# A depthwise convolution shared by two engines: one-tap adds on GpSimd against adds four taps wide

## The chip, the cores and the metric

The kernel runs on one NeuronCore of one Trainium2 chip. The metric is the device time of one execution in microseconds. Three runs of the kernel before took 962.43, 964.1 and 961.76 us; their median is 962.43.

## The reference

A decoder trunk of two layers on 256 positions with 1024 channels, all in float32. Each layer adds half a gated feed-forward network (FFN), a token mixer, and half a second FFN to the residual x; the mixer of the first layer is a pair of convolutions, that of the second is attention. The change lies in the first layer's mixer:

```
def conv_mixers(h, w_in, a_kernel, b_kernel, b_bias, b_ln_g, b_ln_b, w_out):
    z = h @ w_in                                # 1024 -> 2560 channels
    a_b, a_c, a_x, b_val, b_gate = split(z)     # 512 channels each
    y_a = a_b * causal_depthwise_conv(a_c * a_x, a_kernel)          # 3 taps
    u = b_val * sigmoid(b_gate)
    u = causal_depthwise_conv(u, b_kernel) + b_bias                 # 31 taps
    y_b = silu(layer_norm(u, b_ln_g, b_ln_b))
    return concatenate([y_a, y_b]) @ w_out
```

The 31-tap convolution works on each of 512 channels by itself: for every position it is a sum of 31 products, one of each of the last 31 values of u with the channel's weight for that distance.

## The kernel before

Activations lie transposed: 128 channels on the partitions, 256 positions in the free dimension, so a set of 512 channels is four groups of 128x256. Weights come from memory in units of 16 tiles of 128x128 (1 MB, line 116, issued by SyncE), into four buffers. To multiply in float32 accuracy at the faster rate, each unit is split into a rounded part (ScalarE, line 127) and a remainder (VectorE, line 128), and each product is made of three matmuls (lines 163 to 165). A few units, named in WHOLE and the two units for ya, are not split and are used as they are, in a slower matmul (line 161). Such a unit keeps its buffer until TensorE has read it.

The convolution stage (function conv) runs over ten steps p. Each projects a pair of 128-channel groups into a PSUM bank. Steps 0 to 3 give value and gate of the 31-tap convolution, one group c each; VectorE and ScalarE make u[c] from them (lines 499 to 502). Steps 4 to 7 give the two factors of the 3-tap convolution (lines 515 to 529, result ya), steps 8 and 9 its outer gate (lines 538 and 539). Then the first half of the output projection multiplies ya (line 161, 64 matmuls), while the layer norm of the other half runs: sums of y over the channels (GpSimd and VectorE, line 561), a matmul with ones for the mean (line 563), subtraction (line 566), squares, a second matmul (line 201), the reciprocal root, its spreading (line 241), gain and SiLU (lines 576 and 578), and a split into two parts ob[0] and ob[1] (lines 187 and 188). The second half of the output projection multiplies ob.

The 31 taps of a group are shared out. VectorE takes the first 31 - POOL_TAPS[c]: the first as one multiply with the bias added (line 453), each further one as one multiply-and-add into a PSUM accumulator (line 464; the last group has a second accumulator, yl, line 460). For the other taps ScalarE makes the product of one tap (line 486, 128x256) in one of PBUFS = 18 buffers and GpSimd adds it to yp (line 487, 128x256); the first is written into yp by ScalarE itself (line 481). Line 473 adds the two parts into y[c], line 470 adds yl into yp.

The order of the work is written out by hand. Two lists, queue_v for VectorE's taps and queue_p for the products with their adds, get a group's entries when its u is there. At the end of step p, PER_POOL[p] entries of queue_p and then PER_STEP[p] of queue_v are put into the program; the closing addition of a group is placed LATE entries into the next group's taps. AHEAD says how far ahead of the projections units are split. A planner then orders each engine's instructions by this program order, in which a part of the layer norm is moved forward by PRIO_LN; after that each engine runs its queue strictly in order.

All tiles of the stage lie in a pool that is open for the stage alone; xg is a copy of the scaled input, read by the unsplit projections, and ob is a pair of tiles of its own.

Of the kernel before, what the change touches and what calls it, by code (L numbers as in the profile page):

```python
# [10 lines left out]
F32 = mybir.dt.float32  # L11
F32R = mybir.dt.float32r
I32 = mybir.dt.int32
AF = mybir.ActivationFunctionType
# [3 lines left out]
P = 128  # L18
D = 1024
S = 256  # L20
DEPTH = 2
FF = 2816
ND = D // P
# [6 lines left out]
KB = 31  # L30
# [3 lines left out]
UT = 16  # L34
NEG = -1e30

POOL_TAPS = [13, 17, 13, 16]
PER_STEP = [9, 8, 7, 8, 8, 8, 9, 8, 9, 10]
PRIO = 0
WHOLE = {9, 2}  # L40
PBUFS = 18
PER_POOL = [6, 8, 2, 6, 6, 9, 6, 4, 8, 9]
XPRIO = 0
AHEAD = [2, 4, 1, 1, 4, 4, 3, 4, 3, 3]
LATE = 15
OUT_AHEAD = [2, 3]
PRIO_LN = 800
WARM = 7
FINE = {13: 4, 14: 4, 6: 4}
PRIO_C = 500  # L50
PRIO_R = 500
# [9 lines left out]
LINE = 1024  # L61
# [33 lines left out]
def trunk(ctx: ExitStack, tc: tile.TileContext, xin, wst, cst, bia, idn, out):  # L95
    nc = tc.nc
# [21 lines left out]
    def split(u):  # L118
# [3 lines left out]
        w2[u] = w2s.tile([P, UT * P], F32R, name="w2")  # L122
        n = max(2, PIECES.get(u, 1), FINE.get(u - first_conv, 1))
        h = UT * P // n
# [29 lines left out]
    def take(n):  # L154
        st = Stream(used[0])
        used[0] += n
        return st
# [251 lines left out]
    def out_half(st, accs, half, o, ds, ahead=(ahead_split,) * 2):  # L409

        for d in ds:
            for k in range(4):
                t = half * 32 + d * 4 + k
                if t % UT == 0:
                    advance(st.u + t // UT, ahead[t // UT % 2])
                mm3(accs[d // 2][:, d % 2], st.tile(t), [a[:, k] for a in o],
                    half == 0 and k == 0 and d % 2 == 0, half == 1 and k == 3, True)
# [4 lines left out]

    def conv(norm, after):
        with tc.tile_pool(name="cp", bufs=1, reuse_waits="tile") as cp, \
                tc.tile_pool(name="cp2", bufs=PBUFS, reuse_waits="tile") as cp2:
            xg = cp.tile([P, ND, S], F32, name="xg")
            with tc.high_priority(offset=XPRIO):
                for k in range(ND):
                    nc.scalar.activation(xg[:, k], x[:, k], AF.Copy,
                                         scale=const[:, norm.col + k:norm.col + k + 1])  # L430
            _, r = norm.end(WIDEC)
            ob = [cp.tile([P, 4, S], F32R, name=f"ob{i}") for i in range(2)]
            u = cp.tile([P, 4, KB - 1 + S], F32, name="u")
            m = cp.tile([P, 4, KA - 1 + S], F32, name="m")
            y = cp.tile([P, 4, S], F32, name="y")
            yp = cp.tile([P, 4, S], F32, name="yp")
# [8 lines left out]
            def tap(c, j):  # L445
                return const[:, C_BK + c * KB + j:C_BK + c * KB + j + 1]

            def taps_v(c):

                acc = ys[c // 2][:, c % 2]  # L450

                def first():
                    nc.vector.tensor_scalar(acc, u[:, c, :S], tap(c, 0),
                                            const[:, C_BB + c:C_BB + c + 1],
                                            op0=ALU.mult, op1=ALU.add)
                yield first
                for j in range(1, KB - POOL_TAPS[c]):
                    def one(j=j):
                        if c in TWO and j == 1:
                            nc.vector.tensor_scalar_mul(yl[:, TWO.index(c)], u[:, c, j:j + S],  # L460
                                                        tap(c, j))
                            return
                        o = yl[:, TWO.index(c)] if c in TWO and j % 2 else acc
                        nc.vector.scalar_tensor_tensor(o, u[:, c, j:j + S], tap(c, j), o,  # L464
                                                       op0=ALU.mult, op1=ALU.add)
                    yield one

                def last():
                    if c in TWO:
                        nc.vector.tensor_add(yp[:, c], yp[:, c], yl[:, TWO.index(c)])  # L470
                    while any(a <= c for a, _ in queue_p):
                        queue_p.pop(0)[1]()
                    nc.vector.tensor_add(y[:, c], yp[:, c], acc)
                yield last

            def taps_p(c):

                j0 = KB - POOL_TAPS[c]

                def first():  # L480
                    nc.scalar.activation(yp[:, c], u[:, c, j0:j0 + S], AF.Copy, scale=tap(c, j0))
                yield first
                for j in range(j0 + 1, KB):
                    def one(j=j):
                        t = cp2.tile([P, S], F32, name="prod")
                        nc.scalar.activation(t, u[:, c, j:j + S], AF.Copy, scale=tap(c, j))  # L486
                        nc.gpsimd.tensor_add(yp[:, c], yp[:, c], t)  # L487
                    yield one

            queue_v, queue_p, late = [], [], None  # L490
            st = take(10)
            for p in range(10):
                advance(st.u + p, AHEAD[p])
                bank = project(st, p * UT, norm.xs, xg)
                c = p % 4
                with tc.high_priority(offset=PRIO):
                    if p < 4:
# [3 lines left out]
                        nc.scalar.activation(sg, v[:, 1], AF.Sigmoid)  # L501
                        nc.vector.tensor_mul(u[:, c, KB - 1:], v[:, 0], sg)
                        new = list(taps_v(c))
                        held_last, late = late, new.pop()
                        queue_v += new[:LATE] + [f for f in [held_last] if f] + new[LATE:]
                        queue_p += [(c, f) for f in taps_p(c)]
                    elif p < 8:
                        t = tmp.tile([P, S], F32, name="g")
# [5 lines left out]
                        else:  # L514
# [4 lines left out]
                                             scale=const[:, ka:ka + 1])  # L519
                        for j in range(1, KA):  # L520
                            w = const[:, ka + j:ka + j + 1]
                            if T_POOL[c]:
                                t = tmp.tile([P, S], F32, name="sl")
# [6 lines left out]
                    else:  # L530
                        c = 2 * (p - 8)
# [8 lines left out]
                if p == TABLE:  # L540
                    nc.scalar.activation(rsq[:, :1], m[:, 3, KA - 1:KA], AF.Silu)
                for _ in range(min(len(queue_p), PER_POOL[p])):
                    queue_p.pop(0)[1]()
                    if ROBIN and queue_p:
                        a = queue_p[0][0]
                        i = next((i for i, f in enumerate(queue_p) if f[0] != a), None)
                        if i is not None:
                            queue_p.insert(0, queue_p.pop(i))
                for _ in range(min(len(queue_v), PER_STEP[p])):
                    queue_v.pop(0)()  # L550
            for f in queue_v + [late]:
                f()

            st = take(4)
            accs = [psa.tile([P, 2, S], F32, name="pa") for _ in range(4)]
            out_half(st, accs, 0, [ya], range(8), OUT_AHEAD)
            with tc.high_priority(offset=PRIO_LN):
# [16 lines left out]
                _, rs = rsqrt_of([sq2], CM, LN_EPS)  # L574
                for c in range(4):
# [3 lines left out]
                                         scale=const[:, C_LG + c:C_LG + c + 1],  # L579
# [129 lines left out]
    for lo, hi in START:  # L709
        c = slice(2 * lo * P, 2 * hi * P)  # L710
# [4 lines left out]
    cold = psb.tile([P, P], F32, name="pb")  # L715
    for _ in range(WARM):
        nc.tensor.matmul(cold, ones, ones, start=True, stop=True)
# [13 lines left out]
    with tc.tile_pool(name="fp", bufs=1, reuse_waits="tile") as fp:  # L731
# [6 lines left out]
        _, r = rsqrt_of([last.sums, last.sq], D, RMS_EPS, eps)  # L738
        for i, (lo, hi) in enumerate(GROUPS):
            n = hi - lo  # L740
# [93 lines left out]
```

## Time and profile before

| | |
|---|---|
| median of three runs | 962.43 us (961.76 to 964.1) |
| the profiled execution | 960.91 us, of which the span of the trace is 958.8 |
| TensorE (PE) | busy 944.7 us, 99% |
| VectorE (DVE) | busy 731.8 us, 76% |
| ScalarE (ACT) | busy 548.9 us, 57% |
| GpSimd (POOL) | busy 47.9 us, 5%, 61 instructions |
| memory | 174.23 MB read, 183 GB/s over the span |

Engines run side by side, each through its own queue. A busy share is an average over stages with different limits: GpSimd's 5% lies almost wholly in one stretch of 50 us of the convolution stage, from about 204 to 258 us, where it is busy nine tenths of the time. A line of the timeline gives start, duration, engine, line, operation, what it writes and reads, how many instructions are merged, and in brackets how long the engine was idle before and who released it. Merged durations include what lies between the first start and the last end. A matmul's duration includes its way through the pipeline, so consecutive ones overlap.

### The profile page before, as it was taken

The numbers are of one execution on the slowest core, as the hardware profiler recorded it, in microseconds if no ns is written. First come the engines' busy times: TensorE is split into PE (matmuls) and PEld (weight loads), VectorE is DVE, ScalarE is ACT, GpSimd is POOL, SyncE is SP. The second block draws the span as 40 slices with busy tenths as digits, with TensorE's granted clock in tenths as the row PEclk, the third lists the DMA queues.
The fourth block names the chain that finished last, engine by engine and source line by source line (L and its number), as shares of the span: only waits on it lengthen the run. The fifth ranks groups of instructions, "written<-read, shape, count | busy, mean of one in ns | idle before, by whom it ended". The sixth has DMA issues, their size and how long they took to land.

```text
span 958.8 us, 15184 instructions
## 1 busy us (share of the span) xinstructions
PE 944.7 (99%) x5860; PEld 847.1 (88%) x5860; DVE 731.8 (76%) x1383; ACT 548.9 (57%) x985; POOL 47.9 (5%) x61
## 2 busy tenths in 40 slices
PE   9999999999899999999999999999999999999996
PEld 8988898999798888988988889898888998889886
DVE  8988776688999888766788877665698798787552
ACT  6665654497366665544466565444666565665540
POOL 0000000049600000000000000000000000000000
PEclk9999999999999999999999999999999999999998
DMA  9865565543175555555455555556553455555501
GB/s 337 290 213 177 184 212 176 191 161 133 45 284 186 203 204 176 187 209 176 176 201 195 178 197 197 179 201 212 187 198 123 157 184 189 200 194 179 200 17 44
DMA packets 27288, 176.26 MB, mean 184 GB/s; under 512 B 3024, under 2 KB 3792, under 8 KB 6864
## 3 DMA queue, kind: packets, MB, share of 16 engines
q1 hardware_dynamic: 26784, 174.67, 52.2%
q8 instruction: 46, 0.75, 0.3%
q10 hardware_dynamic: 432, 0.63, 0.2%
q14 instruction: 26, 0.21, 0.1%
HBM read 174.23 MB, written 1.05 MB: 183 GB/s over the span
## 4 chain that ended last, share of the span: by engine, by line
PE 91%; DVE 3%; ACT 2%; POOL 1%; issue 1%; DMA 0%; SPq 0%; DVEq 0%; POOLq 0%; ACTq 0%
PE pa L169 33%; PE pa L170 17%; PE pb L169 15%; PE pb L170 8%; PE pa L163 4%; PE pa L164 4%; PE pa L165 4%; PE pa L161 2%; ACT prod L486 1%; DVE pb L464 1%; PE pb L163 1%; PE pb L164 1%; PE pb L165 1%; POOL yp L487 1%; DVE w L128 1%
## 5 line engine op out<-in xcount | busy, mean ns | idle before, releaser
L128 DVE TENSOR_TENSOR w<-raw,w 128x1024 fp32r<-128x1024 f32 (+1 forms) x322 | 381.5, 1196 | 133.6 <-ACT w L127 133.0
L169 PE MATMUL pa<-xs,w 128*128 128x512 f32 x1376 | 479.1, 391 | 0.0
L127 ACT CAST w<-raw 128x1024 fp32r<-128x1024 f32 (+1 forms) x322 | 325.0, 1027 | 134.3 <-PE pa L169 50.0
L170 PE MATMUL pa<-xs,w 128*128 128x256 f32 x1376 | 387.6, 282 | 0.0
L169 PEld LDWEIGHTS pa<-xs,w 128*128 128x128 f32 x1376 | 258.3, 188 | 54.8 <-DVE xs L191 0.5
L170 PEld LDWEIGHTS pa<-xs,w 128*128 128x128 f32 x1376 | 260.0, 189 | 0.1
L169 PE MATMUL pb<-gs,w 128*128 128x512 f32 x616 | 213.7, 390 | 0.0
L170 PE MATMUL pb<-gs,w 128*128 128x256 f32 x616 | 173.7, 282 | 0.0
L169 PEld LDWEIGHTS pb<-gs,w 128*128 128x128 f32 x616 | 115.6, 188 | 24.1
L170 PEld LDWEIGHTS pb<-gs,w 128*128 128x128 f32 x616 | 116.4, 189 | 0.0
L386 ACT ACTIVATE sl<-v 128x256 f32<-128x256 f32 x88 | 36.8, 418 | 106.0 <-DVE v L341 102.0
L339 ACT COPY sq<-pa 128x256 f32<-128x256 f32 x172 | 63.3, 368 | 30.1 <-PE pa L170 24.9
L164 PE MATMUL pa<-xs,w 128*128 128x256 f32 x272 | 76.2, 281 | 0.1
L163 PE MATMUL pa<-xs,w 128*128 128x256 f32 x272 | 76.2, 282 | 0.0
L165 PE MATMUL pa<-xs,w 128*128 128x256 f32 x272 | 76.1, 280 | 0.0
L340 DVE TENSOR_TENSOR v<-pa,sq 128x256 f32<-128x256 f32 x156 | 65.1, 418 | 0.0
L405 DVE SCALAR_TENSOR_TENSOR x<-pb,x 128x256 f32<-128x256 f32 x60 | 25.4, 423 | 42.5 <-PE pb L170 28.5
L487 POOL TENSOR_TENSOR yp<-yp,prod 128x256 f32<-128x256 f32 x55 | 46.3, 845 | 207.8 <-ACT prod L486 203.8
L190 ACT ACTIVATE xs<-x,const 128x256 fp32r<-128x256 f32 x48 | 24.2, 506 | 54.8 <-DVE x L405 43.0
L341 DVE TENSOR_TENSOR v<-v,rr 128x512 f32<-128x512 f32 x78 | 53.4, 684 | 0.0
L164 PEld LDWEIGHTS pa<-xs,w 128*128 128x128 f32 x272 | 51.5, 189 | 0.5 <-DVE xs L191 0.3
L165 PEld LDWEIGHTS pa<-xs,w 128*128 128x128 f32 x272 | 51.1, 188 | 0.2 <-DVE w L128 0.2
(160 smaller groups left out, 926.5 us busy)
## 6 DMA issues: line engine op xcount, KB each, us to landing
raw<-wst SPq DMA_DIRECT2D x159, 1024.0 KB, 4.8
bt<-bia SPq DMA_DIRECT2D x8, 384.0 KB, 3.6
raw<-wst SPq DMA_DIRECT2D x7, 256.0 KB, 6.0
raw<-wst SPq DMA_DIRECT2D x2, 512.0 KB, 6.0
x<-xin SPq DMA_DIRECT2D x3, 256.0 KB, 4.9
out<-y SPq DMA_DIRECT2D x2, 256.0 KB, 2.5
out<-y ACTq DMA_DIRECT2D x2, 256.0 KB, 2.4
x<-xin SPq DMA_DIRECT2D x2, 128.0 KB, 3.1
```

Of the source, the lines that this page charges most:

```text
L127: nc.scalar.copy(w1[u][:, c], raw[u][:, c])
L128: nc.vector.tensor_sub(w2[u][:, c], raw[u][:, c], w1[u][:, c].bitcast(F32))
L163: nc.tensor.matmul(o, a[0], b[0], start=start, stop=False, skip_group_check=check)
L164: nc.tensor.matmul(o, a[0], b[1], start=False, stop=False, skip_group_check=check)
L165: nc.tensor.matmul(o, a[1], b[0], start=False, stop=stop, skip_group_check=check)
L169: nc.tensor.matmul(o, w[0], b, start=start, stop=False, skip_group_check=True)
L170: nc.tensor.matmul(o[:, 0], w[1], b[:, 0], start=False, stop=stop, skip_group_check=True)
L339: nc.scalar.copy(h, bank[:, 1])
L340: nc.vector.tensor_add(v[:, i], bank[:, 0], h)
L341: nc.vector.tensor_mul(v, v, twice(r))
L386: nc.scalar.activation(sl, v[:, 0], AF.Silu)
L487: nc.gpsimd.tensor_add(yp[:, c], yp[:, c], t)
```

## The change

- GpSimd's share is 18 of 31 taps in each group (before 13, 17, 13 and 16).
- ScalarE makes products four to a tile of 128x1024: the first four go straight into acc, four running sums; each further tile (three of four products, one of two) is added to acc by one GpSimd instruction, of 128x1024 or 128x512. A fold then adds the upper two sums to the lower two (128x512) and these to each other, into yp (128x256).
- There are 4 such product tiles (before 18 of one product each) and 2 of acc.
- queue_p has six entries a group; PER_POOL, PER_STEP and LATE have other values.
- In the closing step, the entries of queue_p are put into the program ahead of line 470's addition instead of behind it, since yp is now written by the fold.
- ob takes the buffer of xg, 960 bytes into it; xg's buffer is 1 KB a partition larger.

```
-POOL_TAPS = [13, 17, 13, 16]
-PER_STEP = [9, 8, 7, 8, 8, 8, 9, 8, 9, 10]
+POOL_TAPS = [18, 18, 18, 18]
+QUAD = 4
+PER_STEP = [6, 6, 5, 6, 6, 6, 6, 5, 5, 5]
-PBUFS = 18
-PER_POOL = [6, 8, 2, 6, 6, 9, 6, 4, 8, 9]
+PBUFS = 4
+PER_POOL = [3, 3, 2, 3, 3, 3, 3, 2, 2, 2]
-LATE = 15
+LATE = 10
+OB_START = 960
...
-            xg = cp.tile([P, ND, S], F32, name="xg")
+            xg = cp.tile([P, ND * S + LINE // 4], F32, name="xg")[:, :ND * S].rearrange(
+                "p (d s) -> p d s", d=ND)
...
-            ob = [cp.tile([P, 4, S], F32R, name=f"ob{i}") for i in range(2)]
...
                 def last():
+                    while any(a <= c for a, _ in queue_p):
+                        queue_p.pop(0)[1]()
                     if c in TWO:
                         nc.vector.tensor_add(yp[:, c], yp[:, c], yl[:, TWO.index(c)])
-                    while any(a <= c for a, _ in queue_p):
-                        queue_p.pop(0)[1]()
                     nc.vector.tensor_add(y[:, c], yp[:, c], acc)
...
+            def products(t, c, j0, n):
+                for i in range(n):
+                    nc.scalar.activation(t[:, i], u[:, c, j0 + i:j0 + i + S], AF.Copy,
+                                         scale=tap(c, j0 + i))
...
                 j0 = KB - POOL_TAPS[c]
+                acc = cp3.tile([P, QUAD, S], F32, name="acc")
                 def first():
-                    nc.scalar.activation(yp[:, c], u[:, c, j0:j0 + S], AF.Copy, scale=tap(c, j0))
+                    products(acc, c, j0, QUAD)
                 yield first
-                for j in range(j0 + 1, KB):
-                    def one(j=j):
-                        t = cp2.tile([P, S], F32, name="prod")
-                        nc.scalar.activation(t, u[:, c, j:j + S], AF.Copy, scale=tap(c, j))
-                        nc.gpsimd.tensor_add(yp[:, c], yp[:, c], t)
+                for j1 in range(j0 + QUAD, KB, QUAD):
+                    def one(j1=j1):
+                        n = min(QUAD, KB - j1)
+                        t = cp2.tile([P, QUAD, S], F32, name="prod")
+                        products(t, c, j1, n)
+                        nc.gpsimd.tensor_add(acc[:, :n], acc[:, :n], t[:, :n])
                     yield one
+                def fold():
+                    h = QUAD // 2
+                    nc.gpsimd.tensor_add(acc[:, :h], acc[:, :h], acc[:, h:])
+                    nc.gpsimd.tensor_add(yp[:, c], acc[:, 0], acc[:, 1])
+                yield fold
...
+            ob = cp.tile([P, ND * S + LINE // 4], F32R, name="xg")[:, OB_START // 4:]
+            ob = [ob[:, i * 4 * S:(i + 1) * 4 * S].rearrange("p (c s) -> p c s", c=4)
+                  for i in range(2)]
```

## Rows read from the trace of the kernel before

**Rows 1.** The page: busy time, share of the span and instructions of each engine.
```profile
PE 944.7 (99%) x5860; PEld 847.1 (88%) x5860; DVE 731.8 (76%) x1383; ACT 548.9 (57%) x985; POOL 47.9 (5%) x61
```

**Rows 2.** Busy time by stretches of the convolution stage; columns in the first line.
```profile
core 0: us, PE busy (x) PEld busy (x) DVE busy (x) ACT busy (x) POOL busy (x), PEclk, DMA share, GB/s
252.10:255.90 3.80, 0.03 (x1) 0.00 (x0) 3.80 (x10) 0.00 (x0) 2.87 (x5) 0.94 0.72 239
255.90:259.20 3.30, 3.28 (x9) 2.70 (x9) 3.30 (x8) 0.00 (x0) 0.72 (x1) 0.55 0.10 42
203.20:230.00 26.80, 26.80 (x204) 25.97 (x203) 25.96 (x51) 26.38 (x60) 23.77 (x28) 1.00 0.43 158
230.00:236.20 6.20, 6.20 (x55) 6.20 (x54) 6.20 (x13) 3.15 (x7) 5.89 (x6) 1.00 0.17 40
236.20:240.50 4.30, 4.30 (x39) 4.30 (x38) 0.01 (x1) 2.95 (x6) 3.83 (x7) 1.00 0.46 192
240.50:257.30 16.80, 13.01 (x76) 11.62 (x75) 16.76 (x40) 4.40 (x7) 13.77 (x19) 0.95 0.19 63
```

**Rows 3.** TensorE's timeline where the projections end.
```profile
245.06 7.07 PE L161 MATMUL pa<-xg,raw 128*128 128x256 f32 x32
255.92 3.45 PE L161 MATMUL pa<-ya,raw 128*128 128x256 f32 x8 [3.79 <-DVE ya L539]
259.20 0.59 PE L563 MATMUL pb<-sums,ones 128*128 128x256 f32 x2
259.63 5.34 PE L161 MATMUL pa<-ya,raw 128*128 128x256 f32 x24
264.81 0.50 PE L201 MATMUL pb<-ones,sums 128*128 128x2 f32 x4
272.42 0.82 PE L163 MATMUL pa<-ob,w 128*128 128x256 f32 x4
```

**Rows 4.** Who waited for whom, 195 to 290 us: total, times, longest.
```profile
ACT prod L486 <- POOL yp L487: 4.4, 8, 1.4
DVE ya L527 <- ACT ya L518: 4.3, 1, 4.3
PE pa L161 <- DVE ya L539: 3.8, 1, 3.8
```

**Rows 5.** VectorE's timeline, 190 to 280 us.
```profile
194.15 0.42 DVE L300 TENSOR_TENSOR sums<-sums,sq 128x256 f32<-128x256 f32 x1
...
231.15 1.21 DVE L128 TENSOR_TENSOR w<-raw,w 128x1024 fp32r<-128x1024 f32 x1
...
235.08 0.41 DVE L516 TENSOR_TENSOR m<-pa,g 128x256 f32<-128x256 f32 x1
...
240.54 0.95 DVE L527 SCALAR_TENSOR_TENSOR ya<-m,const,ya 128x256 f32<-128x256 f32 x1 [4.33 <-ACT ya L518]
...
251.46 2.83 DVE L464 SCALAR_TENSOR_TENSOR pb<-u,const,pb 128x256 f32<-128x256 f32 x7
...
256.51 0.74 DVE L473 TENSOR_TENSOR y<-yp,pb 128x256 f32<-128x256 f32 x2
...
257.82 0.43 DVE L561 TENSOR_TENSOR sums<-sums,y 128x256 f32<-128x256 f32 x1
...
259.90 1.41 DVE L566 SCALAR_TENSOR_TENSOR y<-pb,y 128x256 f32<-128x256 f32 x4
...
261.56 1.22 DVE L128 TENSOR_TENSOR w<-raw,w 128x1024 fp32r<-128x1024 f32 x1
...
263.63 0.41 DVE L573 TENSOR_TENSOR sums<-sums,sq 128x256 f32<-128x256 f32 x1
263.97 0.68 DVE L128 TENSOR_TENSOR w<-raw,w 128x512 fp32r<-128x512 f32 x1
...
272.32 0.75 DVE L188 TENSOR_TENSOR ob<-sl,ob 128x256 fp32r<-128x256 f32 x2
```

**Rows 6.** GpSimd's timeline: the stage, then two shorter windows of it.
```profile
204.19 50.33 POOL L487 TENSOR_TENSOR yp<-yp,prod 128x256 f32<-128x256 f32 x55 [203.75 <-ACT prod L486]
254.48 0.73 POOL L561 TENSOR_TENSOR sums<-y 128x256 f32<-128x256 f32 x1
...
231.15 1.80 POOL L487 TENSOR_TENSOR yp<-yp,prod 128x256 f32<-128x256 f32 x1
...
245.56 8.97 POOL L487 TENSOR_TENSOR yp<-yp,prod 128x256 f32<-128x256 f32 x11
```

**Rows 7.** ScalarE's timeline, 196 to 275 us.
```profile
203.62 2.49 ACT L486 ACTIVATE prod<-u,const 128x256 f32<-128x256 f32 x6
206.02 0.40 ACT L501 ACTIVATE sl<-v 128x256 f32<-128x256 f32 x1
...
209.12 3.30 ACT L486 ACTIVATE prod<-u,const 128x256 f32<-128x256 f32 x8
...
243.54 1.99 ACT L127 CAST w<-raw 128x1024 fp32r<-128x1024 f32 x2
```

## What the time will be

> **What bounds the kernel now.** I read the page first, then the busy time by stretches, then the waits of the convolution stage, then the engines' timelines there. The page has TensorE busy for 944.7 of 958.8 us [rows 1]. A change that touches only the convolution can win only where TensorE stands still or runs slow inside that stage. The stretches [rows 2] show one such place: from 252.1 to 255.9 us TensorE does 0.03 us of work, and from 255.9 to 259.2 its granted clock is 0.55, so it runs mostly at the lower of its two levels after the pause. In these 7.1 us it finishes eight matmuls on ya [rows 3]. At full clock the same matmuls take 0.22 us each (24 in 5.34 us), so 1.8 us. The most that can be won is therefore 7.1 - 1.8 = 5.3 us, or 0.55%.
>
> Who holds TensorE there? The wait list names VectorE, "ya L539", 3.8 us [rows 4]. VectorE is late for two reasons. It is nearly always busy with the taps, 25.96 us of 26.80 from 203.2 to 230 [rows 2], and it stood still once for 4.33 us before line 527 [rows 5]. That pause is a chain: line 527 waited for ScalarE's line 518, which stood in ScalarE's queue behind products that waited 4.4 us in all for GpSimd to give back product buffers [rows 4]. GpSimd itself adds without a pause from 204.19 to 254.52 us, 55 adds in 50.33 us [rows 6]. So three engines are close to their limit at once, and a second chain ends at the same place as the first: last add 254.5, y of the last two groups at 256.5, TensorE's mean of the layer norm (line 563) at 259.20, VectorE's line 566 at 259.90 and the first ob at 272.32 [rows 3, 5]. TensorE ends its ya matmuls at 272.4. It needs ob the moment ob is there. Removing the wait for ya alone would only uncover the wait for ob.
>
> **The change part by part.**
>
> *VectorE loses taps.* It had 18 + 14 + 18 + 15 = 65 and gets 4 x 13 = 52. A tap occupies it for 0.40 us from start to start (seven in 2.83 us, the last one's drain included) [rows 5], so 13 x 0.40 = 5.2 us go. The 4.33 us pause should go as well. The product tiles hold 16 products where there were 18, but the work is spread evenly, two or three steps of four products for each projected pair, and the ya of the second pair now stands behind 44 products. The last four of these need the buffer of GpSimd's first add of the second group, done at about 221.5 (206.8, the start worked out below, 12.3 for a group with its share of disturbance, 2.4 for the add), while line 516 of that pair came at 235.08 [rows 5]. VectorE needed until 257.25 for y; with 9.5 us less it could be done near 247.7, when the bank for line 538 of the last pair isn't there yet (the plain matmuls of that pair end at 252.1 [rows 2, 3]). VectorE is off the path then, and TensorE's wait for ya goes: the eight matmuls of channel groups 0 and 1 cover the 1.3 us of lines 538 and 539 for the other two. Next late is y of the last group, that is, GpSimd.
>
> *ScalarE gains products.* 59 become 72, 13 x 0.40 = 5.2 us more [rows 7]. It was busy 26.38 of 26.80 us up to 230, but then 3.15 of 6.20, 2.95 of 4.30 and 4.40 of 16.80 [rows 2]: it had run ahead of GpSimd by its 18 buffers. GpSimd needs 8 products at its start, 26 when it turns to the second group, 44 for the third; ScalarE had made 22 by 212.3 us [rows 7], and GpSimd turns to its second group at about 219. I cost it at nothing; without that cover it is at most these 5.2 us.
>
> *GpSimd adds in other pieces.* For each group 18 taps are four products straight into the running sums, three adds of 128x1024, one of 128x512, and a fold of one 128x512 and one 128x256: six instructions, 24 in all for the 55. The trace has GpSimd at 128x256 only: 11 adds in 8.97 us where nothing disturbs, 0.815 us from start to start of which 0.74 is the add [rows 6]. What a wide one costs has to be bounded. Below: a wide add costs no more than a narrow one, 24 x 0.815 = 19.6 us. Above: strictly by columns, 2.96 and 1.48 us, a group 3 x 2.96 + 2 x 1.48 + 0.74 + 6 x 0.075 = 13.0, in all 52.1 us. The nearest rows are VectorE's, which does the same kind of operation at all three widths: 0.42, 0.68 and 1.22 us [rows 5], so 0.27 per 256 columns and 0.15 fixed. Carrying over the fixed 0.15 us gives GpSimd 2.51 and 1.33 us; carrying over VectorE's ratios (2.91 and 1.62) gives 2.15 and 1.20. I take the middle, 2.33 and 1.27. A group is 3 x 2.33 + 2 x 1.27 + 0.74 + 0.45 = 10.7 and the four are 42.9 us, against 55 x 0.815 = 44.8 before. So the four-fold adds carry 22% more taps in about the same time.
>
> The Trainium skill, "GPSIMD Engine Reference" (Performance versus the Vector engine), states 4497 ns for a 2048-column fp32 add; a line from the 0.74 us row to it gives an estimate of 2.35 us for 1024 columns, and the sum by it would be 43.2 us. No run here shows that width. The page's section When to use GPSIMD advises against it for two-input elementwise work, as about half as fast as VectorE; by the rows above a GpSimd tap is 0.815 us before and would be about 0.60 after, against VectorE's 0.40.
>
> *GpSimd is slowed by VectorE's splits.* The 50.33 us hold 5.5 us more than 55 x 0.815. One add beside a 128x1024 split of line 128 took 1.80 us instead of 0.74 [rows 6, 5]. The eight splits in GpSimd's stretch stay. The next unit's two splits, cast by ScalarE at 243.5 [rows 7] and subtracted only from 258.77 on because VectorE was behind, can now fall before GpSimd's end: 2 x 1.06 us at most, nothing at least; I take 1.0.
>
> *GpSimd starts later.* It started 1.0 us after the first product, at 204.19. Now it needs eight: from 203.21 on, 0.40 apart with one sigmoid among them [rows 7], so at 206.8.
>
> *The end of GpSimd's work.* 206.8 + 42.9 + 5.5 + 1.0 = 256.2, 1.7 us later than the 254.5 of before.
>
> *From there to the layer norm.* VectorE's lines 470 and 473 (0.8 us), its sum (0.43) and line 563 (0.6) put line 566, with the handovers between them, 2.0 us behind GpSimd's end [rows 3, 5] if GpSimd's own two sums (0.73 each [rows 6]) were placed earlier, 2.65 if they stand behind the fold. That is 258.2 to 258.9, against 259.90: 1.0 to 1.7 us earlier. From line 566 to ob the work is unchanged, 12.4 us.
>
> *The clock.* TensorE still pauses, now ahead of line 563 instead of ahead of ya, so a slow stretch like that of 255.9 to 259.2 (a loss of 3.3 - 1.8 = 1.5 us) falls on the 24 matmuls between lines 563 and 201. VectorE's last square sum was done at 264.04 and line 201 came at 264.81 [rows 3, 5], so the chain there already waits 0.75 us for TensorE, and the slow stretch adds between 0 (if the planner puts more ya matmuls ahead of line 563) and 1.5. I take 0.75.
>
> *ob in xg's space, LATE, the order in last().* ob is written at 271 us or later, and xg's last reader ends at 252.1 [rows 3], so that wait is nothing; the pools' sizes change by 1 KB a partition and nothing outside the stage moves. The first three groups are folded many us before VectorE asks for them. Nothing for all three.
>
> **Sum.** 1.35 - 0.75 = 0.6 us gained. The profiled execution took 960.9 us (span 958.8), 1.5 below the median of 962.43; 960.3 on its scale is 961.8 on the median's. That is no change: what 0.3% (2.9 us) does not exceed can't be told from nothing here.
>
> **Rivals.**
>
> *GpSimd's wide adds are cheaper than the middle* (the ratio end or below). At 2.15 and 1.20 us the four groups are 40.2 us, GpSimd ends at 253.5, line 566 starts near 255.8: 4.1 us earlier, less the clock's 0.75, 3.3 us gained, 959.1. Below 1.9 us for a wide add the pause is gone, and the whole 5.3 us: 957.1. For it: each instruction removed saves its fixed part, and 31 of 55 are removed. Against it: VectorE's fixed part is only 0.15 us.
>
> *GpSimd becomes the bound and the kernel is slower.* The place is GpSimd's queue, the price that of the 128x1024 add, and the point from which it decides is 2.6 us (1.38 for the half): 47.0 us of adds, an end at 260.3, line 566 at 262.6, 2.7 us later and with the clock over 3. At the upper bound, 2.96 us, GpSimd ends at 265.4, line 566 at 267.7, and the time is 962.4 + 7.8 + 0.75 = 971. For it: it gets 4352 columns a group, 17,408 against 14,080 before, and it was the engine without a pause. Against it: no engine here is without a fixed part.
>
> *ScalarE starves GpSimd.* Products and casts share one queue that was 98% busy up to 230, and a wide add waits for the last of four products. If a pair of casts (2.0 us [rows 7]) stands ahead of a product once in each of two groups, GpSimd ends 2 to 4 us later: 963.8 to 966. Against it: the even spread.
>
> **How the numbers follow.** Forecast, no change by a near balance: 0.38. Cheaper wide adds: 0.34. GpSimd the bound: 0.16. Starved: 0.12, half of it beyond 0.3%. So faster 0.34, same 0.44, slower 0.22. The forecast's own range is 960 to 965. The range of 8 in 10 goes from 956.8, the whole prize, to 967.5, within the third case, which leaves out its upper end.
>
> **What would show it.** Right: VectorE's pause before line 527 gone and TensorE no longer waiting for ya; a wait of 4 to 5 us before line 563 instead; GpSimd without a pause from about 206.8 to 256; a 128x1024 add at 2.2 to 2.5 us. The middle value is wrong if the wide add is under 2.1 or over 2.6. Starving shows as GpSimd's idle time put down to line "prod" on ScalarE. If TensorE still waits for ya, the reading of VectorE was wrong.

## The result: 1.3% slower, and what the profile after shows

The changed kernel takes 974.63 us (974.27 to 975.22) beside 962.1 us for the kernel before: a ratio of 1.0131, with a 95% interval of 1.0119 to 1.0142. I had forecast no change, 961.8, with 967.5 as the upper end of the range. The profiled execution has a span of 972.8 us, 14.0 more than before.

The page's first part after: TensorE (PE) is busy 1.6 us longer than before [rows 1], so most of the 14 us are waiting. VectorE (DVE) has 13 instructions fewer and is busy 7.9 us longer.
```profile
PE 946.3 (97%) x5860; PEld 847.5 (87%) x5860; DVE 739.7 (76%) x1370; ACT 553.1 (57%) x998; POOL 47.6 (5%) x30
```
Busy time by stretches of the convolution stage after, columns in the first line, beside [rows 2]:
```profile
core 0: us, PE busy (x) PEld busy (x) DVE busy (x) ACT busy (x) POOL busy (x), PEclk, DMA share, GB/s
203.20:230.00 26.80, 26.80 (x204) 25.97 (x203) 26.07 (x40) 23.55 (x55) 22.13 (x12) 1.00 0.24 86
248.70:264.20 15.50, 0.03 (x1) 0.00 (x0) 13.39 (x26) 6.23 (x12) 12.15 (x9) 0.62 0.00 0
264.20:269.60 5.40, 5.36 (x13) 4.29 (x14) 3.72 (x8) 1.50 (x4) 0.00 (x0) 0.50 0.56 187
```
TensorE stands for 15.5 us where it stood for 3.8, and then runs 5.4 us at the lower level of its clock. In the first line VectorE is as busy as before but with 40 instructions instead of 51. Why, the groups of instructions by line and shape between 203 and 263 us show (count, then busy time and mean ns of one). First the kernel before, then the one after:
```profile
L128 DVE TENSOR_TENSOR w<-raw,w 128x1024 fp32r<-128x1024 f32 x6 | 7.6, 1266 | 0.0
L527 DVE SCALAR_TENSOR_TENSOR ya<-m,const,ya 128x256 f32<-128x256 f32 x8 | 5.4, 677 | 4.3 <-ACT ya L518 4.3
L128 DVE TENSOR_TENSOR w<-raw,w 128x512 fp32r<-128x512 f32 x4 | 3.3, 820 | 0.0
L502 DVE TENSOR_TENSOR u<-v,sl 128x256 f32<-128x256 f32 x4 | 2.4, 600 | 0.7 <-ACT sl L501 0.6
L464 DVE SCALAR_TENSOR_TENSOR pb<-u,const,pb 128x256 f32<-128x256 f32 x60 | 27.5, 479 | 0.4
```
```profile
L543 DVE SCALAR_TENSOR_TENSOR ya<-m,const,ya 128x256 f32<-128x256 f32 x8 | 8.9, 1114 | 0.0
L130 DVE TENSOR_TENSOR w<-raw,w 128x1024 fp32r<-128x1024 f32 x5 | 8.8, 1799 | 0.0
L130 DVE TENSOR_TENSOR w<-raw,w 128x512 fp32r<-128x512 f32 x4 | 8.7, 2240 | 0.0
L518 DVE TENSOR_TENSOR u<-v,sl 128x256 f32<-128x256 f32 x4 | 3.1, 765 | 0.5 <-ACT sl L517 0.5
L467 DVE SCALAR_TENSOR_TENSOR pb<-u,const,pb 128x256 f32<-128x256 f32 x47 | 21.2, 481 | 0.4
```
Four kinds of VectorE instruction became longer, and in each both inputs lie in SBUF, the on-chip memory of the tiles (PSUM is where the matmuls write their sums). Undisturbed they take 1.22 and 0.68 us (the splits [rows 5]), 0.475 (the ya sums) and 0.42 (u). What all these instructions take beyond that I call the stretch; summed over the single instructions of 203 to 263 us it is 3.2 us before and 15.6 after. So VectorE lost 12.4 us more, where it was to save 5.2. The taps (line 464 before, 467 now), with one input in SBUF and one in PSUM, kept their 0.48 us.

The timelines show the coincidence. First six splits of VectorE, with the last of them, which took 3.42 us, also by itself; then GpSimd's adds:
```profile
221.08 13.75 DVE L130 TENSOR_TENSOR w<-raw,w 128x512 fp32r<-128x512 f32 x6
231.42 3.42 DVE L130 TENSOR_TENSOR w<-raw,w 128x1024 fp32r<-128x1024 f32 x1
```
```profile
207.09 8.83 POOL L497 TENSOR_TENSOR acc<-acc,prod 128x1024 f32<-128x1024 f32 x4 [206.65 <-ACT prod L481]
230.37 3.38 POOL L497 TENSOR_TENSOR acc<-acc,prod 128x1024 f32<-128x1024 f32 x1
239.07 7.64 POOL L497 TENSOR_TENSOR acc<-acc,prod 128x1024 f32<-128x1024 f32 x3 [5.32 <-ACT prod L481]
252.18 2.35 POOL L497 TENSOR_TENSOR acc<-acc,prod 128x1024 f32<-128x1024 f32 x1
259.84 0.72 POOL L503 TENSOR_TENSOR yp<-acc 128x256 f32<-128x256 f32 x1
```
An undisturbed 128x1024 add takes 2.35 us. The one that began at 230.37 ended at 233.75, and VectorE's split that began at 231.42 ended at 234.84, 1.1 us after it: the split, 1.22 us long by itself, stood until GpSimd was nearly done. GpSimd's add took 3.38 us, 1.0 more than undisturbed, so it lost time as well. GpSimd now also pauses once, for 5.32 us. ScalarE's timeline says why: its queue stood 8.62 us before a ya product, which needed VectorE's line 532, late behind the six splits; GpSimd's next products were behind it.
```profile
235.87 0.51 ACT L534 ACTIVATE ya<-m,const 128x256 f32<-128x256 f32 x1 [8.62 <-DVE m L532]
236.28 1.03 ACT L129 CAST w<-raw 128x1024 fp32r<-128x1024 f32 x1
237.22 4.11 ACT L481 ACTIVATE prod<-u,const 128x256 f32<-128x256 f32 x10
```
So GpSimd ends at 260.56 instead of 254.5 [rows 6], and the mean of the layer norm (line 563 before, 582 now) comes at 264.24 instead of 259.20 [rows 3]. Between the two, VectorE's queue holds other work ahead of the last sums, a split and lines 554 and 555 (0.68 us each):
```profile
260.59 0.42 DVE L475 TENSOR_TENSOR yp<-yp,pb 128x256 f32<-128x256 f32 x1 [2.11 <-POOL yp L503]
260.93 1.39 DVE L130 TENSOR_TENSOR w<-raw,w 128x1024 fp32r<-128x1024 f32 x1
```
TensorE's timeline from there, and below it VectorE's line for the first part of ob:
```profile
245.77 2.97 PE L163 MATMUL pa<-xg,raw 128*128 128x256 f32 x13
264.24 1.22 PE L582 MATMUL pb<-sums,ones 128*128 128x256 f32 x2 [15.51 <-DVE sums L580]
265.25 5.78 PE L163 MATMUL pa<-xg,raw 128*128 128x256 f32 x16
270.87 0.50 PE L203 MATMUL pb<-ones,sums 128*128 128x2 f32 x4
271.23 0.68 PE L163 MATMUL pa<-xg,raw 128*128 128x256 f32 x2
271.75 4.91 PE L163 MATMUL pa<-ya,raw 128*128 128x256 f32 x22
286.01 0.47 PE L165 MATMUL pa<-xg,w 128*128 128x256 f32 x1
279.50 0.76 DVE L190 TENSOR_TENSOR xg<-sl,xg 128x256 fp32r<-128x256 f32 x2 [0.15 <-ACT xg L189]
```
Line 582 now stands in TensorE's queue ahead of the last 18 matmuls of the last projection (the traced rows have 16 and 2) and of all 64 on ya. Before, only 56 were behind it. From the mean to the first matmul on ob (named xg now, at 286.01) it takes 21.8 us instead of 13.2: 26 more matmuls of 0.22 us are 5.7, and 5.4 us at half clock are 2.7. The layer norm isn't what holds TensorE here: the first part of ob is there at 280.26, 5.75 us before TensorE has worked off its queue. Of the 13.8 us by which the second FFN starts later, 5.0 come ahead of the mean and 8.8 behind it.

### The profile page after: what moved, and what is told of

Read it like the earlier page. It is cut to its first block, busy times and chain, and to the rows that moved or that the text cites. A ratio compares the mean times of both kernels' runs of the same rounds, so it can differ in the third digit from the quotient of the medians.

```text
span 972.8 us, 15111 instructions
## 1 busy us (share of the span) xinstructions
PE 946.3 (97%) x5860; PEld 847.5 (87%) x5860; DVE 739.7 (76%) x1370; ACT 553.1 (57%) x998; POOL 47.6 (5%) x30
## 4 chain that ended last, share of the span: by engine, by line
PE 91%; DVE 3%; ACT 2%; POOL 2%; issue 1%; DMA 0%; SPq 0%; POOLq 0%; DVEq 0%; ACTq 0%
PE pa L171 32%; PE pa L172 17%; PE pb L171 14%; PE pb L172 8%; PE pa L165 4%; PE pa L166 4%; PE pa L167 4%; PE pa L163 2%; POOL acc L497 1%; DVE w L130 1%; PE pb L165 1%; PE pb L166 1%; PE pb L167 1%; ACT prod L481 1%; PE pa L355 1%
## 5 line engine op out<-in xcount | busy, mean ns | idle before, releaser
L130 DVE TENSOR_TENSOR w<-raw,w 128x1024 fp32r<-128x1024 f32 (+1 forms) x322 | 389.9, 1224 | 134.7 <-ACT w L129 134.3
L171 PEld LDWEIGHTS pa<-xs,w 128*128 128x128 f32 x1376 | 258.3, 188 | 54.8 <-DVE xs L193 0.5
L172 PEld LDWEIGHTS pa<-xs,w 128*128 128x128 f32 x1376 | 260.0, 189 | 0.1
L341 ACT COPY sq<-pa 128x256 f32<-128x256 f32 x172 | 63.3, 368 | 29.7 <-PE pa L172 25.6
L166 PEld LDWEIGHTS pa<-xs,w 128*128 128x128 f32 x272 | 51.5, 189 | 0.5 <-DVE xs L193 0.3
L167 PEld LDWEIGHTS pa<-xs,w 128*128 128x128 f32 x272 | 51.1, 188 | 0.2 <-DVE w L130 0.2
L165 PEld LDWEIGHTS pa<-xs,w 128*128 128x128 f32 x272 | 51.0, 188 | 0.3
```

The source lines that it names most:

```text
L130: nc.vector.tensor_sub(w2[u][:, c], raw[u][:, c], w1[u][:, c].bitcast(F32))
L165: nc.tensor.matmul(o, a[0], b[0], start=start, stop=False, skip_group_check=check)
L166: nc.tensor.matmul(o, a[0], b[1], start=False, stop=False, skip_group_check=check)
L167: nc.tensor.matmul(o, a[1], b[0], start=False, stop=stop, skip_group_check=check)
L171: nc.tensor.matmul(o, w[0], b, start=start, stop=False, skip_group_check=True)
L172: nc.tensor.matmul(o[:, 0], w[1], b[:, 0], start=False, stop=stop, skip_group_check=True)
```

## The experiments

Two theories. **The port** (a name for a way into SBUF that the two engines would share; the runs show who waits, not the wiring): a GpSimd add and a VectorE instruction with both inputs in SBUF keep each other out, each for its whole length; wide adds make each wait of VectorE longer. **Its rivals:** 18 taps a group are simply too many for GpSimd; or the loss is the planner's, which put the mean too early into TensorE's queue. "The stretch" is the sum defined above throughout.

**e1, the pair by itself.** A small kernel runs GpSimd adds alone and beside VectorE instructions of several kinds.

> A small kernel that does nothing of the reference but move x: GpSimd adds of three widths alone, then beside VectorE operations of five kinds, one section after another. Port theory (a GpSimd add and a VectorE instruction with two inputs in SBUF keep each other out, each for its whole length): beside 128x1024 adds a VectorE 128x512 add of two SBUF inputs takes up to 2.4 + 0.6 = 3.0 us instead of 0.68, beside 128x256 adds up to 1.3 us; multiply-and-adds into PSUM, adds with one PSUM input and operations with one SBUF input keep their lengths (within 0.05 us). Rival (they share the port element by element): all two-input adds slow down by the same factor, some 1.5 to 2, whatever the width of GpSimd's add. Second rival (the stretch comes from something else in the kernel): VectorE keeps 0.68 us throughout.

Its instructions by the tile they write (number, then minimum, median and maximum in ns): gA to gC are GpSimd alone at three widths, vD is VectorE alone, gE/vE, vF, vG, vH and vI run against GpSimd adds, all of 128x1024 but vF's, which are of 128x256.
```profile
L130 POOL TENSOR_TENSOR gAa<-gAa,gAb x4: 721/722/722, 36.5 to 38.9; 128x256 f32<-128x256 f32 x4
L130 POOL TENSOR_TENSOR gBa<-gBa,gBb x4: 1259/1262/1262, 42.0 to 46.0; 128x512 f32<-128x512 f32 x4
L130 POOL TENSOR_TENSOR gCa<-gCa,gCb x4: 2337/2337/2338, 49.6 to 56.8; 128x1024 f32<-128x1024 f32 x4
L133 DVE TENSOR_TENSOR vDa<-vDa,vDb x6: 692/692/693, 61.4 to 65.0; 128x512 f32<-128x512 f32 x6
L130 POOL TENSOR_TENSOR gEa<-gEa,gEb x4: 2666/2668/2762, 68.0 to 76.4; 128x1024 f32<-128x1024 f32 x4
L133 DVE TENSOR_TENSOR vEa<-vEa,vEb x8: 691/1701/2711, 67.9 to 81.1; 128x512 f32<-128x512 f32 x8
L133 DVE TENSOR_TENSOR vFa<-vFa,vFb x8: 691/1095/1096, 84.0 to 91.5; 128x512 f32<-128x512 f32 x8
L135 DVE SCALAR_TENSOR_TENSOR po<-vGa,vGb,po x16: 490/490/490, 100.2 to 108.1; 128x256 f32<-128x256 f32 x16
L138 DVE TENSOR_TENSOR vHa<-pt,vHb x12: 691/691/691, 112.2 to 120.1; 128x512 f32<-128x512 f32 x12
L140 DVE TENSOR_SCALAR vIa<-vIb x12: 426/427/2445, 124.1 to 137.2; 128x512 f32<-128x512 f32 x12
```
The same VectorE add of 0.69 us takes 2.71 beside a wide GpSimd add and 1.10 beside a narrow one; with one input in PSUM (vH), or as a tap (vG), it isn't touched. Beside 128x512 adds it takes 1.63. The wait follows the width of the other engine's instruction, so this isn't an even sharing. One part of the expectation was wrong: not every operation with one SBUF input keeps its length. The 128x512 tensor_scalar from SBUF to SBUF (vI), 0.43 us by itself, was shut out as well, to 2.45, and so was a copy of the same size.

**e2, TensorE's queue alone.** Lowering the layer norm's priority moves the mean behind the projection and four ya matmuls.
```diff
-PRIO_LN = 800
+PRIO_LN = 45
```


> The changed kernel with PRIO_LN 45 instead of 800. TensorE's queue then has the whole last projection and 4 of the 64 ya matmuls ahead of the matmul of line 582; the queues of the other engines are unchanged up to there. Theory (two causes: VectorE late behind GpSimd's long adds, and TensorE's queue, in which line 582 stands ahead of 18 matmuls of the last projection and all of ya): line 582 still comes near 264.5, but ob's matmuls start some 14 us after it instead of 22: 966 to 968 us, so about 7 of the 12.5 us are the queue's. Rival (the late y alone is the cause, the queue costs nothing): 974 to 975. Second rival (the queue is all of it): 962.

974.38 us, ratio 1.0131 [1.0112, 1.015]: nothing won, and my expectation missed. TensorE now waited for ya, which VectorE had at 264 as well, and then the layer norm was held by something new; two lines of who waited for whom, 245 to 290 us (total, times, longest):
```profile
ACT w L129 <- DMA raw<-wst: 19.5, 2, 15.5
PE pa L163 <- DVE ya L555: 11.3, 1, 11.3
```
ScalarE's squares stood behind a cast whose weights were still to come. The unit was loaded into a buffer that VectorE's late split gives back. So with VectorE this late, another order by itself wins nothing: one wait takes the other's place. What the order alone costs this run doesn't tell, since the wait for weights came with it.

**e3, narrow adds with 18 taps.** Each add issued as adds of 128x256, all else as changed.
```diff
-                        nc.gpsimd.tensor_add(acc[:, :n], acc[:, :n], t[:, :n])
+                        for i in range(n):
+                            nc.gpsimd.tensor_add(acc[:, i], acc[:, i], t[:, i])
...
-                    nc.gpsimd.tensor_add(acc[:, :h], acc[:, :h], acc[:, h:])
+                    for i in range(h):
+                        nc.gpsimd.tensor_add(acc[:, i], acc[:, i], acc[:, h + i])
```


> The changed kernel with each add of GpSimd issued as adds of 128x256 (68 instead of 24), the same products, buffers and list entries; TensorE's queue is that of the changed kernel. Port theory: VectorE's six splits that took 13.75 us at 221 shrink to 7 to 9 us, the multiply-and-adds of line 543 that took 2.2 us to 0.9 or less; but GpSimd has 68 x 0.815 = 55 us of adds and ends near 268 instead of 260.6, so the time is 978 to 983. Rival (the stretch comes from the number of taps or from the order, not from the width): the six splits still take 13 to 14 us.

976.56 us, 1.0152 [1.0137, 1.0167], somewhat less than I had put it. The groups between 203 and 263 us:
```profile
L130 DVE TENSOR_TENSOR w<-raw,w 128x1024 fp32r<-128x1024 f32 x5 | 8.1, 1648 | 0.0
L545 DVE SCALAR_TENSOR_TENSOR ya<-m,const,ya 128x256 f32<-128x256 f32 x8 | 5.0, 625 | 4.7 <-ACT ya L536 4.7
L130 DVE TENSOR_TENSOR w<-raw,w 128x512 fp32r<-128x512 f32 x4 | 4.3, 1131 | 0.0
```
The six splits took 7.65 us instead of 13.75, the stretch is 6.2 instead of 15.6: the width makes most of it. The time is no better because GpSimd has 68 adds and ends at 262.76 (not at 268, as I expected), with VectorE waiting 8.6 us for it.

**e4, no shared inputs.** The splits, u and the ya sums take one input from PSUM while GpSimd adds (for the splits a column there, broadcast); the values computed are not the reference's, and the splits no longer depend on ScalarE's casts.
```diff
-            nc.vector.tensor_sub(w2[u][:, c], raw[u][:, c], w1[u][:, c].bitcast(F32))
+            nc.vector.scalar_tensor_tensor(w2[u][:, c], raw[u][:, c], 1.0,
+                                           dummy[0].to_broadcast([P, h]),
+                                           op0=ALU.mult, op1=ALU.subtract)
...
-                        nc.vector.tensor_mul(u[:, c, KB - 1:], v[:, 0], sg)
+                        nc.vector.tensor_mul(u[:, c, KB - 1:], bank[:, 0], sg)
...
-                                    ya[:, c], m[:, c, j:j + S], w, ya[:, c],
+                                    ya[:, c], m[:, c, j:j + S], w, yl[:, 1],
```


> The changed kernel in which VectorE's splits, line 518 and the multiply-and-adds of ya take one input from PSUM instead of SBUF while GpSimd adds (other values are computed; the same number and shape of instructions). TensorE's queue has the whole last projection and 2 ya matmuls ahead of the mean, as in e2. Port theory: no VectorE instruction is stretched, the splits keep 0.68 and 1.22 us, GpSimd's 128x1024 adds 2.35 us each, GpSimd ends at 251 to 253, TensorE hardly waits: 957 to 960. Rival (GpSimd's load of 72 taps is the cause): GpSimd still ends at 258 or later and the time is that of e2, 966 or more.

960.36 us, 0.9982 [0.9973, 0.9992]. The groups between 203 and 263 us:
```profile
L505 POOL TENSOR_TENSOR acc<-acc,prod 128x1024 f32<-128x1024 f32 x12 | 28.8, 2396 | 209.9 <-ACT prod L489 209.4
L132 DVE SCALAR_TENSOR_TENSOR w<-raw,pb 128x1024 fp32r<-128x1024 f32 x9 | 10.7, 1211 | 0.0
L551 DVE SCALAR_TENSOR_TENSOR ya<-m,const,pb 128x256 f32<-128x256 f32 x8 | 3.8, 475 | 1.7 <-ACT ya L542 1.6
L132 DVE SCALAR_TENSOR_TENSOR w<-raw,pb 128x512 fp32r<-128x512 f32 x4 | 2.7, 678 | 0.0
L563 DVE TENSOR_TENSOR ya<-ya,v 128x512 f32<-128x512 f32 x2 | 2.9, 1474 | 0.0
```
The last line is a multiply of ya whose two inputs the edit left in SBUF: the one of the two that stood beside a GpSimd add took 2.25 us, the other 0.69. So in the same kernel the exclusion goes on where both inputs are in SBUF.

With the same 72 taps on GpSimd and the same widths, the stretch of the four kinds is 0.5 us and 14.3 us of time are gone. e2 has nearly the same queue on TensorE and the loss in full, so neither the queue nor the number of taps accounts for it without the port. That the splits no longer wait for ScalarE is a second change in this run; e9 doesn't make it. GpSimd ended later than I had put it, at 255.2, and began 2.7 us later than in the changed kernel; that may be why the time lies just above the expected 957 to 960.

**e5, wide adds with the old shares.** The four running sums and the folds stay.
```diff
-POOL_TAPS = [18, 18, 18, 18]
-PER_STEP = [6, 6, 5, 6, 6, 6, 6, 5, 5, 5]
-PER_POOL = [3, 3, 2, 3, 3, 3, 3, 2, 2, 2]
-LATE = 10
+POOL_TAPS = [13, 17, 13, 16]
+PER_STEP = [9, 8, 7, 8, 8, 8, 9, 8, 9, 10]
+PER_POOL = [3, 3, 2, 3, 2, 2, 2, 2, 1, 1]
+LATE = 15
```


> The changed kernel with GpSimd's shares and VectorE's step counts of the kernel before (13, 17, 13, 16 taps, LATE 15): only the width of the adds is changed. TensorE's queue has the mean behind 8 ya matmuls, as before. Port theory: GpSimd has only some 35 us of adds and ends before 250, yet VectorE's two-input instructions are stretched by 9 to 15 us (3.2 before), it finishes its taps later than before, and the time is 965 to 969. Rival (18 taps a group are too much for GpSimd, the width costs nothing): with the old shares the wide adds win, 957 to 961.

966.56 us, 1.005 [1.0035, 1.0065]. GpSimd was done with its taps at 249.24, 5 us sooner than before, and the stretch was 11.3 us. TensorE waits for ya:
```profile
260.21 3.78 PE L163 MATMUL pa<-ya,raw 128*128 128x256 f32 x8 [6.54 <-DVE ya L555]
263.78 0.72 PE L582 MATMUL pb<-sums,ones 128*128 128x256 f32 x2
289.40 0.40 PE L171 MATMUL pa<-xs,w 128*128 128x512 f32 x1
```
So with GpSimd early, the wide adds (with the four sums and folds that go with them) cost 4.5 us. Together with e3 this is a square, though its first corner, the kernel before, has one running sum and other buffers: narrow and old shares 962.0, wide and old shares 966.6, narrow and 18 taps 976.6, wide and 18 taps 974.6. In it the shares cost more than the width: with wide adds 8 us of the loss come only with 18 taps. That these 8 us, too, need the exclusion is what e4 shows, which has 18 taps and wide adds and no loss. The mean is as late here (263.78) as in the changed kernel, but with the queue of before the second FFN starts 25.6 us after it (line 171) instead of 32.3.

**e6, ob in tiles of its own**, as before.
```diff
-            ob = cp.tile([P, ND * S + LINE // 4], F32R, name="xg")[:, OB_START // 4:]
+            ob = [cp.tile([P, 4, S], F32R, name=f"ob{i}") for i in range(2)]
```


> The changed kernel with ob in tiles of its own, as before; all queues are as in the changed kernel. All theories: nothing, 974.6 within 1 us. If ob's place in xg's buffer cost a wait, up to 3 us less.

975.04 us, 1.0138 [1.0123, 1.0153]: ob's place costs nothing.

**e7, the kernel before with 26 buffers**, in the space that ob gives free.
```diff
-PBUFS = 18
+PBUFS = 26
```


> The kernel before with ob in xg's buffer and the freed space used for 26 product buffers instead of 18; nothing else. If VectorE's 4.33 us pause came from products waiting for GpSimd's buffers, it goes, y is there up to 2 us earlier, limited by GpSimd's end at 254.5: 959.5 to 961.5. Rival (the pause hides under GpSimd anyway): 962.

961.18 us, 0.9987 [0.9977, 0.9997]. VectorE's 4.33 us pause is gone and ya no longer waited for; TensorE now waits 3.9 us for the mean instead, because GpSimd ends no sooner than it did (255.5). It is the fastest kernel here that computes the reference, by 0.8 us, which is too little to be called a gain.

**e8, adds two taps wide with the old shares.**
```diff
-POOL_TAPS = [18, 18, 18, 18]
-QUAD = 4
-PBUFS = 4
+POOL_TAPS = [13, 17, 13, 16]
+QUAD = 2
+PBUFS = 9
```


> The changed kernel with two running sums instead of four (adds of 128x512), the shares and step counts of the kernel before and 9 product tiles of two; TensorE's queue as in the kernel before. Port theory: one GpSimd add holds VectorE off for up to 1.26 us, so the stretch lies between the 3.2 us of the kernel before and the 9 to 15 of e5, near 6; GpSimd has 39 us of adds and ends near 250, the 4.33 us pause goes: 959.5 to 962.5. Rival (width costs nothing): 957 to 959.

962.07 us, 1.0 [0.999, 1.0009]. The stretch is 8.5 us (I had put it near 6), between e5's 11.3 and the 3.2 of before. GpSimd ends at 250.19 and VectorE's pause goes, but TensorE still waits 5.5 us for ya: the 5.3 us of added stretch are more than the 4.33 of the pause.

**e9, the changed kernel with u and the ya sums taking one input from PSUM**; the reference is computed.
```diff
-                        sg = tmp.tile([P, S], F32, name="sl")
+                        sg = bank[:, 1]
...
-                        nc.scalar.activation(ya[:, c], m[:, c, :S], AF.Copy,
-                                             scale=const[:, ka:ka + 1])
+                        nc.vector.tensor_scalar_mul(yl[:, 1], m[:, c, :S], const[:, ka:ka + 1])
...
-                                    ya[:, c], m[:, c, j:j + S], w, ya[:, c],
+                                    ya[:, c] if j == KA - 1 else yl[:, 1], m[:, c, j:j + S], w, yl[:, 1],
```


> The changed kernel with the sigmoid written back into the projection's PSUM bank and the 3-tap convolution's sum kept in the free half of yl's bank (its first product on VectorE instead of ScalarE), so that lines 518 and 543 have one input in PSUM; the whole reference is computed. The splits still have both inputs in SBUF. TensorE's queue has 4 ya matmuls ahead of the mean, as in e2. Port theory: of the 15.6 us that VectorE lost, the 6.5 of these twelve instructions go, the 9 of the splits stay; GpSimd's 5 us pause shrinks too, since ScalarE no longer waits with ya; the time is 965 to 969. Rival (the port is not it): 974.

967.32 us, 1.0049 [1.0034, 1.0064]: 7.3 us back. Not all of it is VectorE's stretch: the edit also takes ya's first product out of ScalarE's queue, and GpSimd's 5.32 us pause goes (it ends at 257.03). The mean stands behind the projection and four ya matmuls, as in e2. u and the ya sums have no stretch left; the splits keep theirs, 11.3 us over eleven of them:
```profile
L130 DVE TENSOR_TENSOR w<-raw,w 128x1024 fp32r<-128x1024 f32 x7 | 13.6, 1968 | 0.0
L130 DVE TENSOR_TENSOR w<-raw,w 128x512 fp32r<-128x512 f32 x4 | 8.6, 2186 | 0.1
```

**e10, e11, e12: can the port's knowledge be turned into a win?** e8 and e7 with e9's two operands in PSUM, and e9 with 16 taps a group.
```diff
-POOL_TAPS = [18, 18, 18, 18]
-PER_STEP = [6, 6, 5, 6, 6, 6, 6, 5, 5, 5]
+POOL_TAPS = [16, 16, 16, 16]
+PER_STEP = [7, 7, 6, 7, 7, 7, 7, 6, 6, 6]
```


> e8 with the same two operands in PSUM. Port theory: of e8's 8.5 us, 4.9 go, VectorE ends its taps near 256 instead of 260; but the queue now has 28 ya matmuls ahead of the mean, so the layer norm starts at 258.5 and ob comes near 271.5: 959.5 to 961.5. Rival (nothing gained): 962.

> e7 (one-tap adds, 26 buffers) with the same two operands in PSUM: only 1.8 of its 2.6 us can go, and GpSimd's end near 254 stays: 960 to 962.

> e9 with 16 taps a group on GpSimd (three 128x1024 adds and the fold, no 128x512 remainder) and 15 on VectorE. GpSimd has 38 us of adds, ends near 251; VectorE loses 8 to 9 us to the port in its splits; the mean stands behind 18 ya matmuls: 959 to 963. Rival (16 taps are still too many): 965 or more.

965.91 (1.0041 [1.0027, 1.0056]), 963.8 (1.0015 [1.0005, 1.0024]) and 965.73 us (1.0039 [1.0025, 1.0053]): all three slower than I had put them, though the stretch fell to 4.6 us in e10 and 1.6 in e11 (9.0 in e12, as expected). e12's time is that of its rival, by which 16 taps are still too many (965 or more); but GpSimd ends at 251.09 there, as the port theory had it, and then waits 6.5 us for VectorE, so GpSimd's load isn't what is late. In e10 and e11 the planner puts 28 ya matmuls ahead of the mean; TensorE then runs dry at the layer norm's last matmuls (line 243 in e10), 3.0 and 3.1 us, with none on ya left to cover it. In all three ScalarE waits 18 to 20 us in total for weights between 195 and 290 us, where it was 3.7 in the kernel before. What share of the lost time each of these has no run tells.

## Why the prediction was wrong, point by point

- *The place was right:* the part from the last projection to ob decides, GpSimd's end comes last ahead of the mean, and VectorE's pause before line 527 and TensorE's wait for ya are gone, as forecast.
- *GpSimd's own instructions were right:* 2.35, 1.26 and 0.72 us against 2.33, 1.27 and 0.74, a start at 207.09 against 206.8. GpSimd ended at 260.56 all the same, not at 256.2. The second rival, "GpSimd becomes the bound", had the right sign, but by a price (2.6 us or more) that the add alone doesn't have. The third, "ScalarE starves GpSimd", gave its sign, idle time of GpSimd put down to "prod" on ScalarE; but behind it stood a ya product that waited for VectorE, not casts, and its 963.8 to 966 was too low as well. The prediction's range ended too low for want of any other cause on that side.
- *The step that failed is "GpSimd is slowed by VectorE's splits".* I had the row for it, one add of 1.80 us beside a split [rows 6], and read it one way only: as GpSimd's loss, 1.0 us more. For GpSimd the term was large enough: its adds took 46.2 us where 24 undisturbed ones are 41.2, so it lost 5.0, and the prediction had 5.5 + 1.0. But it was an exclusion, and VectorE pays for it with the length of GpSimd's instruction; that side the prediction put at nothing. It measured 12.4 us (15.6 - 3.2); e1 shows the pair alone, e4 and e9 that the time follows it. That these 12.4 us and the 12.5 us of lost time are nearly equal is chance: the taps saved and the pause gone stand against the one, and TensorE's queue has a part in the other.
- *"VectorE loses taps ... VectorE is off the path" failed with it.* It saved 5.2 us of taps and lost 12.4, so it finished its taps at 258.5 instead of about 248.
- *"ScalarE gains products ... I cost it at nothing" missed 5.3 us.* The even spread was there, but ScalarE's queue holds a product of ya, and that waits for VectorE. GpSimd's pause follows; without it GpSimd would have ended near 255.2 (an estimate, 260.56 - 5.32), no later than forecast.
- *"From there to the layer norm" was too short.* From GpSimd's end to the layer norm's subtraction (line 566 before, 585 now) it took 4.9 us instead of 2.0 to 2.65, since VectorE, behind with its work, did a split and lines 554 and 555 in between.
- *"From line 566 to ob the work is unchanged, 12.4 us", and "The clock", which had the pause ahead of line 563 cost 0 to 1.5 us, took the queue behind it as before.* The planner put the mean ahead of 82 matmuls instead of 56, and TensorE came to ob 20.5 us after the subtraction began. That the tail grew by 8.8 us is measured, and that its matmuls and clock add up to it is worked out. How much the queue alone costs stays open: e2, made to isolate it, put a wait for weights in its place, and e5, with the old queue and an equally late mean, differs in its shares too.
- *ob, LATE and the order in last():* ob's place costs nothing, as predicted (e6). The other two no run tries by themselves.

The Trainium skill, "SBUF — State Buffer" (Who interferes with whom), states that GpSimd's port pair is VectorE's second one and is held for a whole instruction, also against a VectorE instruction with two SBUF inputs. The traces here agree: 2.71 us instead of 0.69 beside a 128x1024 add, 0.69 with one input in PSUM. By that rule a split beside a GpSimd add has to be charged up to 2.35 us on VectorE's side, and the prediction didn't weigh it.

## What to carry to other kernels

When two engines exclude each other per instruction, a longer instruction on the helper is a longer wait on the main engine; saving the helper's fixed costs is then paid by the other side. Price both sides: for every instruction of the main engine that can meet the lock, up to one whole instruction of the helper. What can be freed is an operand: with one of the two inputs in PSUM the instructions tried here left the contest (0.69 and 0.49 us in e1), though the order of the queues that follows has to be checked again (e10 and e11 had less stretch and yet were slower than e8 and e7).

## What the runs showed of the hardware that I had not expected

- The two engines take turns one for one: in e1 each of four wide GpSimd adds (2.67 us, 2.34 alone) alternates with one of VectorE's adds (2.71, 0.69 alone); neither starves.
- A one-input 128x512 tensor_scalar from SBUF to SBUF, which runs in 0.43 us, is shut out in the same way (2.45 us).
- GpSimd's fp32 add is a line through 0.72, 1.26 and 2.34 us: 0.54 us per 256 columns and 0.18 fixed.
